# Head norm weight as a row, one product for the output gate, and an earlier start for splitting the feature sums

## The chip, the cores and the metric

The kernel runs on one core of one Trainium2 chip. The metric is the device time of one execution in microseconds (us). Before the change the median of three runs is 1377.43 us (1377.10 to 1377.72).

## The reference

One encoder layer over 1024 tokens of width 1024, in float32. What the change touches is in the first half of it:

```python
h = rmsnorm(x, norm_mix[l])
proj = h @ w_in[l]
q, k, v, r, lr_f, lr_b, u, g_a, g_b = jnp.split(proj, split_points, axis=-1)
...
o = o_fwd + o_bwd                                   # gated linear attention, 4 heads of 256 values
o = o * lax.rsqrt(jnp.mean(o * o, axis=-1, keepdims=True) + EPS)
o = o.transpose(0, 2, 1, 3).reshape(bsz, length, GLA_VALUE_DIM) * gla_norm[l].astype(jnp.float32)
o = (o * jax.nn.silu(r.astype(jnp.float32))).astype(x.dtype)
y_a = o @ w_branch_gla[l]
```

After it come a pooling branch, a gated merge of the two branches, an output projection, and a SwiGLU feed-forward part.

## The kernel before

**Number format.** Every large product is made of three: each float32 operand is split into a high part, which ScalarE rounds (`split_to`, L201, names ending in `h`), and a low part, the difference, which VectorE or GpSimd subtracts (L202, names ending in `l`). TensorE then adds high times high, high times low and low times high into one PSUM bank (L274).

**Order of the work.** The program is written by hand, in the order in which each engine runs it. `pump` (L162) is called once per three products and counts them. A list of generators stands beside the main line, and each is advanced when its count has run down. `beside` (L685) is one of them: at each step it issues loads (SyncE's queue), casts a high part (L708, `trh`) for the job of the step before, and subtracts the low part (L699, `trl`) of the cast before that. What a step yields is the number of product triples until its next step.

**Stages around the change.** The attention of head h runs beside the projections. When one half of the tokens of a head is done, `turn` (L991) multiplies each token's row of `o` (token on the partition, 256 values in the row) by that token's norm (L997), transposes blocks of 32 by 32 on VectorE (L998) and stores the result to DRAM (`o_out`). The projection of r follows, feature tile by feature tile, j from 0 to 5, with two halves of 512 tokens each; one half is 24 products of TensorE. For each (j, half), `gated` (L1199) takes the silu of r on ScalarE (L1202, `sr`) and multiplies it with the loaded `o` (`ol`) and with the norm's weight, which there is one number per partition (L1212). That product is cut into four instructions of 128x128. Four gated pieces make a block that is stored to DRAM (`ob_out`).

The tiles j = 6 and 7 of r, and the later projections, are computed by a seven-product scheme for 2 x 2 blocks (`Unit`, L1090, and `Gates`, L1475). The first unit runs its products in the order p = 1, 2, 6, 5, 3, 7, of 12 TensorE products each. Its products 1, 2 and 3 use the split activations `hh` and `hl`, which are in SBUF. Products 6, 5, 7 and 4 use sums of activation blocks, which were stored to DRAM earlier (`f_out`). `feature_parts` (L666) loads these eight sums (two for each p, in the order p = 6, 5, 7, 4; `hs`) and lets `beside` split them into `trh` and `trl`. The weights of the unit are loaded as `fraw`; for p = 1 and 2 they are split as they are, for the other p sums of them (`fs`, L1110) are made on VectorE first. Product 6 adds onto the PSUM bank of product 1, so it waits until ScalarE has copied product 1 out (L1497, `ga`).

**Memory.** Nearly all tiles of 512 KB (4 KB per partition) take turns in one pool of 39 slots: a tile's first writer waits for the last reader of the tile that had the slot before.

Of the kernel before, what the change touches and what calls it, by code (L numbers as in the profile page):

```python
# [10 lines left out]
F32 = mybir.dt.float32  # L11
# [4 lines left out]
ALU = mybir.AluOpType  # L16

P = 128
# [7 lines left out]
DV = 256  # L26
# [3 lines left out]
SQ = 32  # L30
# [14 lines left out]
PUT = 3  # L45
# [9 lines left out]
def kernel(  # L55
# [20 lines left out]
    nc = tc.nc  # L76
# [4 lines left out]
    const = ctx.enter_context(tc.tile_pool(name="const", bufs=1))  # L81
# [12 lines left out]
    def name(s):  # L94
        count[0] += 1
        return f"{s}_{count[0]}"

    def slot(dtype=F32, shape=(2, HALF), s="slot"):
        return slots.tile([P, *shape], dtype, tag="slot", name=name(s))

    def t2(width=HALF, dtype=F32, s="t"):
        return tmp.tile([P, width], dtype, tag="t2", name=name(s), padded_shape=[P, HALF + 2 * PAD])
# [7 lines left out]
    def bank(pool, s="ps"):  # L110
        return pool.tile([P, HALF], F32, tag=pool.name, name=name(s))

    def as_f32(ap):
        return ap.bitcast(F32)
# [33 lines left out]
    side, aside = [], []  # L148
# [6 lines left out]
    def soon(delay, *steps):  # L155
        put_off.extend([delay, step] for step in steps)
# [283 lines left out]
    g_mix, g_ffn, g_gla, g_pool = (cols[:, 8 * i : 8 * i + 8] for i in range(4))  # L440
# [118 lines left out]
    def later(dst, src):  # L559
        deferred.append((dst, src))  # L560

    def flush(eng=nc.sync):
        while deferred:
            eng.dma_start(*deferred.pop(0))
# [101 lines left out]
    def feature_parts():  # L666
        todo = [(p, c) for p in (6, 5, 7, 4) for c in range(2)]
        wholes = []

        def load_sum():  # L670
            if len(wholes) < len(todo):
                p, c = todo[len(wholes)]
                wholes.append(slot(s="hs"))
                nc.sync.dma_start(wholes[-1][:, :, :], f_out[p][:, c])

        yield load_sum, None, None
        for n, (p, c) in enumerate(todo):
            yield load_sum, wholes[n][:, :, :], p

    def parts_for(src):  # L680
        if len(src.shape) == 2:
            return [t2(dtype=F32R, s=s)[:, :] for s in ("uph", "upl")]
        return [slot(F32R, s=s)[:, :, :] for s in ("trh", "trl")]

    def beside(jobs, every, put, lag):  # L685

        casts, differ = [None] * lag, None
        puts = [[] for _ in range(put)]
        while True:
            job = next(jobs, None)  # L690
            if not any((job, *casts, differ, *puts)):
                return
            if put:
                for pair in puts.pop(0):
                    nc.sync.dma_start(*pair)
            puts.append([])
            if differ:
                src, (hi, lo), dst = differ
                nc.vector.tensor_tensor(lo, src, as_f32(hi), op=ALU.subtract)  # L699
                if len(src.shape) == 2:  # L700
                    puts[-1] += [(dst[:, i, :], as_f32(t)) for i, t in enumerate((hi, lo))]
                else:
                    right.setdefault(dst, []).append((hi, lo))
            differ, cast = None, casts.pop(0)
            if cast:
                src, dst = cast
                parts = parts_for(src)
                nc.scalar.copy(parts[0], src)  # L708
                differ = src, parts, dst
            casts.append(None)  # L710
            if job:
                op, src, dst = job
                if op:
                    op()
                if src is not None:
                    casts[-1] = src, dst
                elif dst is not None:

                    puts[-1].append((dst, op.args[0]))
            if not put:  # L720
                for pair in puts.pop():
                    nc.sync.dma_start(*pair)
            yield every

    def prepare_beside(jobs, every, put=PUT, lag=1):
        aside.append([beside(chain(*jobs), every, put, lag), every])

    def finish_beside():
        while aside:
# [5 lines left out]
    o_heads, unscaled, last_o = {}, [], []  # L735
# [78 lines left out]
    def attention(h):  # L814
# [113 lines left out]
        def scores(half):  # L928
            sc = [bank(ps_g, "sc") for _ in range(2)]
            for d in range(2):  # L930
                for i in range(4):
                    n = 4 * half + i
                    nc.tensor.matmul(
                        sc[d][:, i * CH : (i + 1) * CH], chunk_of(ke, n, d), chunk_of(qe, n, d),
                        start=True, stop=True,
                    )
            hi, lo = (t2(dtype=F32R, s="p")[:, :] for _ in range(2))
            nc.vector.copy_predicated(sc[1][:, :], keep.rearrange("p n c -> p (n c)"), sc[0][:, :])
            split_to(hi, lo, sc[1][:, :])
            return hi, lo  # L940
# [41 lines left out]
        p = scores(0)  # L982
# [5 lines left out]
        old = sf = None  # L988
        scales, turned = {}, {}

        def turn(half, part):  # L991
            if part == 0:
                turned[half] = slot(shape=(DV // SQ, 4 * SQ), s="ot")
            two = slice(2 * part, 2 * part + 2)
            for i in range(2 * part, 2 * part + 2):
                t = o[half][:, i, :]
                nc.vector.tensor_scalar(t, t, scales[half][:, i : i + 1], None, op0=ALU.mult)  # L997
            nc.vector.transpose(  # L998
                turned[half][:, :, :].rearrange("p k (n b) -> p n k b", b=SQ)[:, two],
                o[half][:, two, :].rearrange("p n (k a) -> p n k a", a=SQ),  # L1000
            )
            if part:
                to = o_out[h][half].rearrange("(k a) (i m) -> i a k m", a=SQ, i=4)
                for i in range(4):
                    (last_o if h == HEADS - 1 else deferred).append((to[i], turned[half][i * SQ : (i + 1) * SQ, :, :]))

        for n in range(NT):
            half, i = n // 4, n % 4
            op = bank(ps_g, "op")
# [21 lines left out]
            if n == 3:  # L1031
                p = q_next
# [166 lines left out]
    def gated(j, half, src):  # L1199

        sr = t2(s="sr")
        nc.scalar.activation(sr[:, :], src, AF.Silu)  # L1202
        if j // 2 not in oT:
            oT[j // 2] = [slot(s="o") for _ in range(2)], []
        tiles, there = oT[j // 2]

        def every(t, i):
            return t.rearrange("p (n i b) -> p i n b", n=4, b=SQ)[:, i]

        turned = o_heads[j // 2][half][:, j % 2, :].rearrange("p (i n b) -> p i n b", i=4, b=SQ)  # L1210
        for i in range(4):
            nc.vector.scalar_tensor_tensor(  # L1212
                every(tiles[half][:, j % 2, :], i), turned[:, i], g_gla[:, j : j + 1], every(sr[:, :], i),
                op0=ALU.mult, op1=ALU.mult,
            )
        there.append((j, half))
        if len(there) == 4:
            c = j // 2 % 2
            for half, t in enumerate(tiles):
                later(ob_out[j // 4, half][:, 2 * c : 2 * c + 2, :], t[:, :, :])  # L1220
            soon(2, flush)
# [8 lines left out]
    for j in range(KT - 2):  # L1230
        if 2 <= j <= 4:
            load_o(j - 2)
        w = take()
        if j == 4:
            for _ in range(2):
                gunits[0].load()
        if j == 5:
            gates_ahead.step()
        if j < BY:
            whole_r = slot(s="r")  # L1240
        for half in range(2):
            if j >= BY and not sums_begun and (j > BY or not side):
                finish_side()
                finish_beside()
                prepare_beside([feature_parts()], 5)
                sums_begun = True
            ps = feature_major(w, hT, half)
            if half == 0:
                flush()
                if j == 4:  # L1250
                    deferred.extend(last_o)
                    flush()
                elif j == 5:
                    load_o(HEADS - 1)
            elif j == KT - 3:
                for _ in range(2):
                    gunits[1].load()
            if j < BY:
                nc.scalar.copy(whole_r[:, half, :], ps[:, :])
                raw_r.append((j, half, whole_r[:, half, :]))  # L1260
            else:
                put_by()
                gated(j, half, ps[:, :])
            if j == KT - 3 and half == 0:
                gates_ahead.step()
# [746 lines left out]
    scales = {}  # L2012
# [74 lines left out]
    for at, p in enumerate(OUT_ORDER):  # L2087
# [9 lines left out]
        for i in range(CLOSE if closing else n_of):  # L2097
            n = at * n_of + i
# [57 lines left out]
```

## Time and profile before

| what | value |
|---|---|
| median of three runs | 1377.43 us |
| the profiled execution's own time | 1377.28 us |
| its span, first to last instruction | 1375.6 us |
| TensorE (PE) busy | 1357.9 us, 99% of the span |
| VectorE (DVE) busy | 861.7 us |
| ScalarE (ACT) busy | 647.2 us |
| GpSimd (POOL) busy | 756.6 us |
| mean granted clock of TensorE | 0.995 |

All times below are microseconds from the start of the span. In a timeline row stand the start, the duration, the engine, the line, the operation, what is written and read, and how many instructions are merged into the row; in square brackets the idle time of the engine before it and what ended it. PE is TensorE, SPq the queue of SyncE that issues the DMAs.

### The profile page before, as it was taken

What the parts mean: (1) busy time and instruction counts of PE and PEld (TensorE: products, weight loads), DVE (VectorE), ACT (ScalarE), POOL (GpSimd) and SP (SyncE); (2) the same over time, 40 slices, a digit from 0 to 9 for tenths busy, and PEclk for the clock granted to TensorE, in tenths of its full rate; (3) what the DMA queues carried; (4) which work ended last, traced back from release to release, by engine and by line L of the source; (5) the groups of instructions that cost most, each with busy time, mean ns of one, the idle gap of its engine ahead of it and who ended that gap; (6) DMA issues with size and microseconds to landing.
All of it is one profiled execution on the core that took longest, in us unless ns stands there. A gap on an engine that the chain in (4) does not pass through costs nothing. (4 is left out here: it accounts for less than half of the span.)

```text
span 1375.6 us, 17848 instructions
## 1 busy us (share of the span) xinstructions
PE 1357.9 (99%) x6246; PEld 1129.0 (82%) x6246; DVE 861.7 (63%) x1102; ACT 647.2 (47%) x1177; POOL 756.6 (55%) x561
## 2 busy tenths in 40 slices
PE   9999999999799999999999999999999999999998
PEld 7888888888688888888888888888888888888886
DVE  6965556657745777688883955656556556343375
ACT  7365666754434445554347533333333334444353
POOL 3323723222487547668665376666666667455454
PEclk9999999999899999999999999999999999999999
DMA  6322523315778578996416355555544447985552
GB/s 226 115 85 55 184 84 93 91 48 170 259 230 281 183 217 302 374 369 221 165 62 245 115 177 176 177 176 177 170 143 136 143 139 266 386 305 185 170 214 77
DMA packets 176987, 254.08 MB, mean 185 GB/s; under 512 B 11608, under 2 KB 102784, under 8 KB 176896
## 3 DMA queue, kind: packets, MB, share of 16 engines
q1 hardware_dynamic: 176752, 252.67, 54.7%
q8 instruction: 49, 0.80, 0.2%
q14 instruction: 42, 0.34, 0.1%
q10 hardware_dynamic: 144, 0.26, 0.0%
HBM read 169.79 MB, written 83.10 MB: 184 GB/s over the span
## 5 line engine op out<-in xcount | busy, mean ns | idle before, releaser
L202 POOL TENSOR_TENSOR wl<-fs,wh 128x512 fp32r<-128x512 f32 x124 | 173.8, 1406 | 163.3 <-ACT wh L201 107.2
L274 PE MATMUL ps<-gh,wh 128*128 128x512 f32 x616 | 240.5, 390 | 0.0
L274 PE MATMUL ps<-gl,wh 128*128 128x512 f32 x616 | 239.8, 389 | 0.3 <-DVE gl L1714 0.3
L274 PE MATMUL ps<-gh,wl 128*128 128x512 f32 x616 | 239.7, 389 | 0.0
L202 POOL TENSOR_TENSOR wl<-fraw,wh 128x512 fp32r<-128x512 f32 x93 | 135.4, 1456 | 74.4 <-ACT wh L201 70.0
L202 POOL TENSOR_TENSOR ol<-gor,oh 128x1024 fp32r<-128x1024 f32 (+1 forms) x42 | 101.6, 2423 | 85.7 <-ACT oh L201 71.1
L274 PE MATMUL ps<-hh,wh 128*128 128x512 f32 x356 | 144.3, 405 | 0.7 <-ACT ga L1497 0.7
L274 PE MATMUL ps<-hl,wh 128*128 128x512 f32 x356 | 138.8, 390 | 0.0
L274 PE MATMUL ps<-hh,wl 128*128 128x512 f32 x356 | 138.8, 390 | 0.0
L274 PEld LDWEIGHTS ps<-gl,wh 128*128 128x128 f32 x616 | 115.7, 188 | 24.3 <-DVE gl L1714 0.7
L274 PEld LDWEIGHTS ps<-gh,wl 128*128 128x128 f32 x616 | 115.6, 188 | 24.2
L274 PEld LDWEIGHTS ps<-gh,wh 128*128 128x128 f32 x616 | 115.7, 188 | 24.0 <-ACT hb L1733 0.3
L274 PE MATMUL ps<-oh,oh 128*128 128x512 f32 x308 | 119.8, 389 | 0.0
L274 PE MATMUL ps<-ol,oh 128*128 128x512 f32 x308 | 119.8, 389 | 0.0
L274 PE MATMUL ps<-oh,ol 128*128 128x512 f32 x308 | 119.8, 389 | 0.0
L202 POOL TENSOR_TENSOR wl<-wraw,wh 128x512 fp32r<-128x512 f32 x56 | 93.4, 1696 | 44.3 <-ACT wh L201 44.2
L202 DVE TENSOR_TENSOR ol<-wor,oh 128x1024 fp32r<-128x1024 f32 (+1 forms) x42 | 62.6, 1501 | 67.8 <-ACT oh L201 55.3
L202 POOL TENSOR_TENSOR wl<-raw,wh 128x512 fp32r<-128x512 f32 x34 | 47.9, 1419 | 85.6 <-ACT wh L201 62.1
L201 ACT CAST wh<-fs 128x512 fp32r<-128x512 f32 x124 | 76.0, 614 | 29.7 <-DVE fs L1110 28.7
L274 PEld LDWEIGHTS ps<-hh,wl 128*128 128x128 f32 x356 | 66.8, 188 | 14.1
L274 PEld LDWEIGHTS ps<-hh,wh 128*128 128x128 f32 x356 | 67.0, 188 | 13.4 <-ACT ga L1497 1.1
L274 PEld LDWEIGHTS ps<-hl,wh 128*128 128x128 f32 x356 | 67.0, 188 | 12.3
(278 smaller groups left out, 3091.1 us busy)
## 6 DMA issues: line engine op xcount, KB each, us to landing
fraw<-in_w_ffn_in_dram SPq DMA_DIRECT2D x44, 512.0 KB, 6.9
gor<-g_out SPq DMA_DIRECT2D x35, 512.0 KB, 7.1
fraw<-in_w_in_dram SPq DMA_DIRECT2D x22, 512.0 KB, 7.5
g_out<-s SPq DMA_DIRECT2D x44, 256.0 KB, 2.0
wor<-t_out SPq DMA_DIRECT2D x20, 512.0 KB, 5.2
raw<-in_w_in_dram SPq DMA_DIRECT2D x36, 256.0 KB, 4.5
g_out<-g SPq DMA_DIRECT2D x33, 256.0 KB, 2.6
x<-in_x_dram SPq DMA_DIRECT2D x16, 512.0 KB, 4.4
```

The source lines that it names most:

```text
L201: nc.scalar.copy(hi, src)
L202: eng.tensor_tensor(lo, src, as_f32(hi), op=ALU.subtract)
L274: nc.tensor.matmul(ps, a[i], b[j], start=first and n == 0, stop=last and n == 2, skip_group_check=onto)
```

## The change

Three edits:

1. `turn` multiplies by the norm's weight too. Each head loads a tile `gain_row`, its 256 weights broadcast to all 128 partitions, by one more DMA; the `tensor_scalar` of L997 becomes a `scalar_tensor_tensor` with that row. The count of instructions stays (32 of 128x256).
2. `gated` has no weight to multiply any more, and its four `scalar_tensor_tensor` of 128x128 become one `tensor_tensor` of 128x512. There are 16 gated pieces, so 64 instructions become 16.
3. The `beside` generator that splits the feature sums takes its first two steps one product triple apart, where all its steps were five apart. Its first step comes after one triple, not five, and all later steps come twelve triples earlier in the program.

```diff
-    def beside(jobs, every, put, lag):
+    def beside(jobs, every, put, lag, quick):
...
-            yield every
-
-    def prepare_beside(jobs, every, put=PUT, lag=1):
-        aside.append([beside(chain(*jobs), every, put, lag), every])
+            quick -= 1
+            yield 1 if quick >= 0 else every
+
+    def prepare_beside(jobs, every, put=PUT, lag=1, quick=0):
+        aside.append([beside(chain(*jobs), every, put, lag, quick), 1 if quick else every])
...
+        gain_row = const.tile([P, DV], F32, tag="gain_row", name=name("gain_row"))
+        nc.sync.dma_start(gain_row[:, :], gla_norm[0:1, h * DV : (h + 1) * DV].broadcast_to([P, DV]))
+
         def turn(half, part):
...
-                nc.vector.tensor_scalar(t, t, scales[half][:, i : i + 1], None, op0=ALU.mult)
+                nc.vector.scalar_tensor_tensor(
+                    t, t, scales[half][:, i : i + 1], gain_row[:, :], op0=ALU.mult, op1=ALU.mult
+                )
...
-        def every(t, i):
-            return t.rearrange("p (n i b) -> p i n b", n=4, b=SQ)[:, i]
-
-        turned = o_heads[j // 2][half][:, j % 2, :].rearrange("p (i n b) -> p i n b", i=4, b=SQ)
-        for i in range(4):
-            nc.vector.scalar_tensor_tensor(
-                every(tiles[half][:, j % 2, :], i), turned[:, i], g_gla[:, j : j + 1], every(sr[:, :], i),
-                op0=ALU.mult, op1=ALU.mult,
-            )
+        turned = o_heads[j // 2][half][:, j % 2, :].rearrange("p (i n b) -> p n i b", i=4, b=SQ)
+        dst, silu = (t.rearrange("p (n i b) -> p n i b", n=4, b=SQ) for t in (tiles[half][:, j % 2, :], sr[:, :]))
+        nc.vector.tensor_tensor(dst, turned, silu, op=ALU.mult)
...
-                prepare_beside([feature_parts()], 5)
+                prepare_beside([feature_parts()], 5, quick=2)
```

The third edit moves instructions on ScalarE and in SyncE's queue. The first place is ScalarE's order between r's fourth tile and the first unit. `trh<-hs` is the cast of a feature sum, `sr` a silu for a gated piece, `wh<-fraw` the cast of the unit's weights for p = 1 and then p = 2. The number behind a name tells tiles apart. Before:

```order
L708 CAST trh_3467<-hs_3400 128x1024
L1202 ACTIVATE sr_3483<-r_2882 128x512
L1202 ACTIVATE sr_3489<-ps_3435 128x512
L708 CAST trh_3511<-hs_3462 128x1024
L1202 ACTIVATE sr_3528<-r_2882 128x512
L1202 ACTIVATE sr_3534<-ps_3497 128x512
L201 CAST wh_3540<-fraw_3431 128x512
L708 CAST trh_3549<-hs_3470 128x1024
L708 CAST trh_3572<-hs_3514 128x1024
L1202 ACTIVATE sr_3587<-r_3015 128x512
L1202 ACTIVATE sr_3593<-ps_3544 128x512
L201 CAST wh_3599<-fraw_3431 128x512
```

With the change, from the third sum's cast on:

```order
L708 CAST trh_3472<-hs_3403 128x1024
L1208 ACTIVATE sr_3491<-r_2888 128x512
L1208 ACTIVATE sr_3494<-ps_3444 128x512
L708 CAST trh_3507<-hs_3424 128x1024
L708 CAST trh_3528<-hs_3475 128x1024
L1208 ACTIVATE sr_3536<-r_2888 128x512
L1208 ACTIVATE sr_3539<-ps_3499 128x512
L201 CAST wh_3542<-fraw_3440 128x512
L708 CAST trh_3562<-hs_3510 128x1024
L1208 ACTIVATE sr_3583<-r_3021 128x512
L1208 ACTIVATE sr_3586<-ps_3546 128x512
L201 CAST wh_3589<-fraw_3440 128x512
```

The cast of the fourth sum (`trh_3572` before, `trh_3507` now) stood behind the p = 1 weights' cast and now stands ahead of it; ahead of the p = 2 weights' cast there were four sums' casts and now there are six. What follows on ScalarE now, up to the copy of product 1 that product 6 waits for, are the casts of the last two sums, two silus, three casts of weight sums and the copy:

```order
L708 CAST trh_3602<-hs_3531 128x1024
L708 CAST trh_3621<-hs_3565 128x1024
L1208 ACTIVATE sr_3634<-r_3021 128x512
L1208 ACTIVATE sr_3637<-ps_3597 128x512
L201 CAST wh_3647<-fs_3595 128x512
L201 CAST wh_3651<-fs_3593 128x512
L201 CAST wh_3661<-fs_3655 128x512
L1497 COPY ga_3681<-ps_3667 128x512
```

The last two sums' casts stood behind that copy before, and stand ahead of it now.

The second place is SyncE's queue in the same stretch. Before:

```order
L674 DMA hs_3514<-f_out_562 128x1024
L674 DMA hs_3552<-f_out_564 128x1024
L564 DMA ob_out_2777<-o_3370 128x1024
L564 DMA ob_out_2778<-o_3371 128x1024
L674 DMA hs_3575<-f_out_564 128x1024
L1050 DMA ol_3583<-o_out_568 128x2x512
L1050 DMA ol_3584<-o_out_568 128x2x512
L674 DMA hs_3621<-f_out_561 128x1024
L674 DMA hs_3642<-f_out_561 128x1024
```

With the change:

```order
L674 DMA hs_3510<-f_out_564 128x1024
L674 DMA hs_3531<-f_out_561 128x1024
L564 DMA ob_out_2783<-o_3378 128x1024
L564 DMA ob_out_2784<-o_3379 128x1024
L674 DMA hs_3565<-f_out_561 128x1024
L1056 DMA ol_3579<-o_out_568 128x2x512
L1056 DMA ol_3580<-o_out_568 128x2x512
```

The last two sums' loads (`f_out_561`) stood behind the load of `ol` and now one stands ahead of the stores `ob_out` and one right behind them.

## The prediction, made before the changed kernel was run

> **What bounds the kernel now.** I read the page first, then the waits of TensorE, then the stretch with the only long wait.
>
> ```profile
> PE 1357.9 (99%) x6246; PEld 1129.0 (82%) x6246; DVE 861.7 (63%) x1102; ACT 647.2 (47%) x1177; POOL 756.6 (55%) x561
> ...
> PE ps L274 <- ACT ga L1497: 7.9, 2, 7.2
> PE op L274 <- DVE p L202: 0.4, 2, 0.2
> ```
>
> TensorE has work for 1357.9 of 1375.6 us. Its largest wait is one of 7.2 us for the copy `ga`; the other of that row (0.7 us) is product 3's wait for the copy of product 5, which the order 5, 3 makes in both kernels. The change can win what this one stall costs and little else. The timeline of TensorE and the windows around it (PE and PEld busy, DVE, ACT, POOL; then the granted clock):
>
> ```profile
> 346.81 0.39 PE L274 MATMUL ps<-hh,wh 128*128 128x512 f32 x1
> 347.04 0.39 PE L274 MATMUL ps<-hl,wh 128*128 128x512 f32 x1
> 347.27 0.39 PE L274 MATMUL ps<-hh,wl 128*128 128x512 f32 x1
> ...
> 351.80 0.39 PE L274 MATMUL ps<-hl,wh 128*128 128x512 f32 x1
> 352.03 0.39 PE L274 MATMUL ps<-hh,wl 128*128 128x512 f32 x1
> 359.66 0.79 PE L274 MATMUL ps<-trh,wh 128*128 128x512 f32 x1 [7.25 <-ACT ga L1497]
> 360.25 0.63 PE L274 MATMUL ps<-trl,wh 128*128 128x512 f32 x1
> 360.68 0.63 PE L274 MATMUL ps<-trh,wl 128*128 128x512 f32 x1
> ...
> 365.37 0.47 PE L274 MATMUL ps<-trl,wh 128*128 128x512 f32 x1
> ...
> 352.20:359.70 7.50, 0.25 (x2) 0.04 (x1) 6.41 (x12) 4.10 (x8) 3.04 (x3) 0.71 1.09 356
> 359.70:365.40 5.70, 5.70 (x14) 4.44 (x15) 2.93 (x6) 3.59 (x6) 5.12 (x3) 0.50 0.85 340
> ```
>
> TensorE's products follow each other by 0.227 us; the 24 of the unit's p = 1 and p = 2 run from 346.81 to 352.26. Product 6 could have started at 352.26 and started at 359.66: 7.4 us. Then the clock stands at 0.50, and products from 360.25 to 365.37 follow by 0.427 us: 13 times 0.2 us, 2.6 us more. The stall is worth 10 us, 0.7%.
>
> Who is late is seen on ScalarE:
>
> ```profile
> 336.63 0.61 ACT L201 CAST wh<-fraw 128x512 fp32r<-128x512 f32 x1
> 337.14 1.05 ACT L708 CAST trh<-hs 128x1024 fp32r<-128x1024 f32 x1
> 344.06 1.05 ACT L708 CAST trh<-hs 128x1024 fp32r<-128x1024 f32 x1 [5.88 <-PE ps L274]
> 345.02 0.63 ACT L1202 ACTIVATE sr<-r 128x512 f32<-128x512 f32 x1
> 345.55 0.58 ACT L1202 ACTIVATE sr<-ps 128x512 f32<-128x512 f32 x1
> 346.03 0.61 ACT L201 CAST wh<-fraw 128x512 fp32r<-128x512 f32 x1
> ...
> 352.02 1.05 ACT L708 CAST trh<-hs 128x1024 fp32r<-128x1024 f32 x1 [3.68 <-DMA hs<-f_out]
> ...
> 358.50 0.62 ACT L201 CAST wh<-fs 128x512 fp32r<-128x512 f32 x1 [3.40 <-DVE fs L1110]
> 359.03 0.58 ACT L1497 COPY ga<-ps 128x512 f32<-128x512 f32 x1
> ```
>
> The copy is short and its input, product 1, is done at 349.5 (346.81 and 12 times 0.227); it stands at the end of a queue that waited for a slot (344.06), for a load (352.02) and for VectorE (358.50). VectorE was late through gated pieces and GpSimd:
>
> ```profile
> 353.63 4.24 DVE L1212 SCALAR_TENSOR_TENSOR o<-ol,cols,sr 128x128 f32<-128x128 f32 x8 [1.09 <-ACT sr L1202]
> ...
> L1212 DVE SCALAR_TENSOR_TENSOR o<-ol,cols,sr 128x128 f32<-128x128 f32 x64 | 28.6, 516 | 13.2 <-ACT sr L1202 10.6 <-POOL wl L202 2.4
> ...
> 358.39 0.68 DVE L1110 TENSOR_TENSOR fs<-fraw,fraw 128x512 f32<-128x512 f32 x1
> 358.99 1.21 DVE L699 TENSOR_TENSOR trl<-hs,trh 128x1024 fp32r<-128x1024 f32 x1
> ```
>
> **The gate as one product.** 64 instructions hold VectorE 28.6 us in this stretch. A 128x512 product of two SBUF tensors takes 0.68 us and the next starts after 0.60 (358.39 to 358.99). 16 of them are 10.9 us: VectorE gets 17.7 us back. The operands' runs stay 32 numbers long; were each product no faster than four old ones at their median of 0.344 us, it would take 1.4 us and still lengthen nothing. By itself this would bring `fs` and the copy nearer, by about 2.9 us of the 4.24 at 353.63. Whether it does depends on what ScalarE waits for.
>
> **The row weight.** No row shows a `scalar_tensor_tensor` of 128x256 from SBUF. The nearest are the old form and the same form from PSUM:
>
> ```profile
> L997 DVE TENSOR_SCALAR o<-o,ors x32: 310/344/1395, 125.7 to 323.6; 128x256 f32<-128x256 f32 x32
> L917 DVE SCALAR_TENSOR_TENSOR st<-kv,fac,so x48: 445/483/486, 97.4 to 317.3; 128x256 f32<-128x256 f32 x48
> ```
>
> So 0.10 to 0.14 us more each, 32 of them: 3.2 to 4.5 us of VectorE from 125 to 325. I cost this at nothing: TensorE works on the projections beside the attention and waits there for VectorE 0.4 us in all, 0.2 at most (the row `op` above). Without that cover it costs up to 4.5 us. Four more DMAs of 128 KB in SyncE's queue are issued long before the first use; behind them stand loads and stores of tiles needed much later. Zero.
>
> **The earlier sums.** The loads, casts and low parts come twelve triples, 8 us, earlier in the program. That gains only where nothing else holds them, and two things do.
>
> First, the slot at 344.06. The fourth sum's cast takes a slot that r's last half-tile (TensorE) still reads; the built program has it wait for the same matmul in both kernels. In the new order the cast of the p = 1 weights, which before ran at 336.63, stands behind it: two casts (0.96 each from start to start), two silus (0.53, 0.48), so it starts at 346.99 and ends at 347.6. TensorE wants it at 346.81: 0.8 us late. Its low part on GpSimd takes 1.29 us more, to 348.9, or to 350.3 if VectorE's low part is ahead of it, where the third product of p = 1 stood at 347.27. **A new stall of 1.6 to 3.1 us opens in front of the old one.** It costs nothing in the sum as long as product 6 still waits longer. The p = 2 weights follow a load that can issue at 344.29 only:
>
> ```profile
> 342.70 0.34 SPq L674 DMA_DIRECT2D hs<-f_out  x1
> 343.09 0.90 SPq L564 DMA_DIRECT2D ob_out<-o  x2
> ...
> 344.29 1.10 SPq L674 DMA_DIRECT2D hs<-f_out  x1
> ...
> DMA to landing us min/median/max: 2.6/3.5/4.4
> ...
> L564 SPq DMA_DIRECT2D ob_out<-o x8: 338/424/3318, 343.1 to 389.8; - x8
> ...
> DMA to landing us min/median/max: 2.6/7.0/8.1
> ```
>
> The first landing row is of the sums' tiles, loads and earlier stores together; the second, with the row above it, is of the `ob_out` stores. With 3.5 us the p = 2 cast runs at 349.8 to 350.4; p = 2 begins at 351.1 to 352.6. In time. Products 1 and 2 end at 353.9 to 355.4.
>
> Second, and this sets product 6: the seventh sum's cast (`trh_3602`) takes the slot of a gated block, and waits until the second `ob_out` store has read it. That store waits for the gated product of the silu at 345.98, done at 347.3, so it issues at 347.4. Its landing takes 2.6 to 8.1 us by the last row; the queue ahead of it is as at 342.70 (a sum's load and a store), with less behind it, so I take 6.4, nearer to the loaded median than to the store that ran alone: **353.8**. From there it is serial, since the eighth cast takes the slot that the seventh low part frees: cast 1.05, low part 1.21, cast 0.96, silu 0.63, on VectorE two gated products and two weight sums (0.60, 0.60, 0.60, 0.68), copy 0.58, releases 0.2: 7.1 us. Product 6 starts at 360.9, 1.2 us later than before.
>
> Its third product needs the low part of its weights. GpSimd is asked for it 4.9 us after the landing, while VectorE runs five two-input instructions without a pause:
>
> ```profile
> 365.91 0.68 DVE L1110 TENSOR_TENSOR fs<-fraw 128x512 f32<-128x512 f32 x1
> 366.51 1.22 DVE L699 TENSOR_TENSOR trl<-hs,trh 128x1024 fp32r<-128x1024 f32 x1
> 367.65 0.68 DVE L1110 TENSOR_TENSOR fs<-fs,fraw 128x512 f32<-128x512 f32 x1
> ...
> 366.37 3.10 POOL L202 TENSOR_TENSOR wl<-fraw,wh 128x512 fp32r<-128x512 f32 x1 [1.55 <-ACT wh L201]
> 369.43 1.29 POOL L202 TENSOR_TENSOR wl<-fs,wh 128x512 fp32r<-128x512 f32 x1
> ```
>
> At 366.37 GpSimd took 3.10 us for what takes 1.29 alone: it got on when VectorE's row ended at 368.3. Blocked so until 361.3, the low part ends at 362.6, 1.9 us after the old 360.68; if it slips in between, the lateness stays 1.2. I take 1.5. [...]
>
> **The sum**, on the profiled execution's 1377.28 (its median of three runs is 1377.43, 0.15 higher): gate 0, row 0, sums +1.5, clock as before 0: **1378.8 us, +0.1%**. Measurement here tells 0.2%, 2.75 us, from no change, so I call it no change: the stall moves from a load to a store. Bounds of the term: the store at 2.6 us, with ScalarE free from 350.4, gives 357.5, 2.2 us sooner; 8.1 us gives 362.6 and with the blocked GpSimd 3.6 later.
>
> **Rivals.**
> - *The stall goes* (0.05). If the casts' slots come free earlier than I read from the built program, all eight sums are split before 352. 1377.3 - 7.4 - 2.6 = 1367.3. For it: VectorE has the time. Against: the 5.88 us wait at 344.06, which an earlier request only lengthens.
> - *The store lands quickly* (0.12). 2.6 us, 2.2 gained; the idle stretch is then too short for the slow clock, 2.6 more: 1372.5. Against: two more transfers leave within 1 us of it.
> - *The clock stays up* (0.20). My idle stretch is 5.5 to 7 us, broken by the two halves of the new stall, against 7.4 in one piece, of which the clock at 0.71 says that it fell after about 3 (3.1 us at 1 and 4.4 at 0.5 make 0.71). Without the slow products 1378.8 - 2.6 = 1376.2, still no change. [...]
> - *The store is late: slower* (0.16). At 8.1 us, GpSimd blocked: 1377.3 + 3.6 = 1380.9. It decides from a landing of 7.4 us on (354.8, plus 8.8 to the third product, 2.9 late). For it: the median of 7.0 is close.
> - *The longer row instruction reaches TensorE* (0.05): up to 1377.3 + 4.5 = 1381.8. Against: no wait of TensorE on VectorE above 0.2 us there.
>
> My forecast itself has 0.42. Faster: 0.17 (the first two). Same: 0.42 + 0.20 = 0.62. Slower: 0.21. The range 1373.0 to 1381.3 leaves out the vanished stall, about half of the quick store and the top of the last.
>
> **What would show it.** Right: TensorE idle in two places, some 0.8 us at 346.8 and 1 to 2 us right behind it, released by the p = 1 weights (`wh`, then `wl`), where it had no gap; then 5 to 7 us up to about 361, released by the copy or by `wl`; ScalarE waiting at 344.06 with the p = 1 cast after it, and for an `ob_out` store near 353.8; gated products of 0.68 us, VectorE's total some 14 us lower. Wrong: no gap at 346.8; product 6 before 357 or after 363; a gap of TensorE above 1 us before 340.

## The result, and the profile after

The changed kernel takes 1383.41 us (median of five runs, 1383.05 to 1384.54), the kernel before, on the same chip, 1377.43 (1377.10 to 1377.79). The ratio is 1.0046, 95% interval 1.0031 to 1.0060: **slower by 6.0 us**, where I had forecast 1378.8 and a range up to 1381.3. The profiled execution of the change took 1384.49 us, its span is 1382.7 (1375.6 before); it is 1.1 us above its median.

The busy times on the page of the changed kernel:

```profile
PE 1358.9 (98%) x6246; PEld 1128.5 (82%) x6246; DVE 857.4 (62%) x1054; ACT 647.3 (47%) x1177; POOL 754.5 (55%) x561
```

Its waits of TensorE (us in total, times, longest):

```profile
PE ps L274 <- ACT ga L1497: 10.7, 2, 9.9
PE ps L274 <- POOL wl L202: 2.3, 4, 0.9
...
PE ps L274 <- ACT wh L201: 0.7, 1, 0.7
```

TensorE is busy for 1358.9 us (1357.9 before): of the 7.1 us between the two spans 1.0 is busy time, and the rest is waiting. The wait for the copy `ga` has grown from 7.2 to 9.9 us, and there are small waits for weights, `wl` and `wh`, that were not there. The timeline of TensorE in r's stage, after the change:

```profile
349.28 0.50 PE L274 MATMUL ps<-hh,wh 128*128 128x512 f32 x1 [0.67 <-ACT wh L201]
...
350.76 0.50 PE L274 MATMUL ps<-hh,wl 128*128 128x512 f32 x1 [0.75 <-POOL wl L202]
...
366.71 0.80 PE L274 MATMUL ps<-trh,wh 128*128 128x512 f32 x1 [9.94 <-ACT ga L1497]
```

Product 6 starts at 366.71, where it started at 359.66. ScalarE's timeline shows the order that it waits through:

```profile
345.70 2.01 ACT L708 CAST trh<-hs 128x1024 fp32r<-128x1024 f32 x2 [9.57 <-PE ps L274]
...
348.62 0.61 ACT L201 CAST wh<-fraw 128x512 fp32r<-128x512 f32 x1
349.70 1.05 ACT L708 CAST trh<-hs 128x1024 fp32r<-128x1024 f32 x1 [0.47 <-DMA hs<-f_out]
...
357.38 1.04 ACT L708 CAST trh<-hs 128x1024 fp32r<-128x1024 f32 x1 [5.11 <-DMA ob_out<-o]
359.72 1.04 ACT L708 CAST trh<-hs 128x1024 fp32r<-128x1024 f32 x1 [1.29 <-DVE trl L699]
...
364.32 0.62 ACT L201 CAST wh<-fs 128x512 fp32r<-128x512 f32 x1 [1.52 <-DVE fs L1116]
366.07 0.59 ACT L1497 COPY ga<-ps 128x512 f32<-128x512 f32 x1 [1.13 <-DVE fs L1116]
```

The casts at 345.70 are the fourth and fifth of the sums, then come the sixth (349.70), the seventh (357.38) and the eighth (359.72), and only then the copy. Before, the seventh and eighth stood behind it:

```profile
359.03 0.58 ACT L1497 COPY ga<-ps 128x512 f32<-128x512 f32 x1
...
360.03 1.05 ACT L708 CAST trh<-hs 128x1024 fp32r<-128x1024 f32 x1
...
361.50 1.04 ACT L708 CAST trh<-hs 128x1024 fp32r<-128x1024 f32 x1
```

Of the 7.05 us by which product 6 is later, 1.64 are there already at the fourth cast (345.70 to 344.06). Most of those are one wait of TensorE in the attention:

```profile
167.52 0.50 PE L274 MATMUL ps<-wl,hh 128*128 128x512 f32 x1 [0.94 <-POOL wl L202]
```

The profile of before has no wait there, but it isn't the row's: the runs below with the gate alone and with the sums alone have it too (0.69 and 1.06 us), and the row alone has no more of it (0.63). What is left, 5.4 us, arises between the fourth cast and product 6.

### The profile page after: what moved, and what is told of

It is laid out like the page before. It is cut to its first block, busy times and chain, and to the rows that moved or that the text cites. A ratio compares the mean times of both kernels' runs of the same rounds, so it can differ in the third digit from the quotient of the medians.

```text
span 1382.7 us, 17799 instructions
## 1 busy us (share of the span) xinstructions
PE 1358.9 (98%) x6246; PEld 1128.5 (82%) x6246; DVE 857.4 (62%) x1054; ACT 647.3 (47%) x1177; POOL 754.5 (55%) x561
## 5 line engine op out<-in xcount | busy, mean ns | idle before, releaser
L274 PE MATMUL ps<-trh,wh 128*128 128x512 f32 x176 | 69.6, 396 | 9.9 <-ACT ga L1497 9.9
```

The lines of the kernel that those rows point to most:

```text
L274: nc.tensor.matmul(ps, a[i], b[j], start=first and n == 0, stop=last and n == 2, skip_group_check=onto)
```

## The experiments

All times are medians; each ratio is to the kernel before, timed on the same chip (1377.5 to 1377.75), with its 95% interval.

### The three parts apart

**The row alone:** the changed kernel, sums as before, the gate in its four old pieces with a constant.

```diff
-                every(tiles[half][:, j % 2, :], i), turned[:, i], g_gla[:, j : j + 1], every(sr[:, :], i),
+                every(tiles[half][:, j % 2, :], i), turned[:, i], 1.0, every(sr[:, :], i),
```

> The kernel before with the head norm's weight as a row alone: the row is loaded and multiplied in as the head's output is scaled, the gate stays in four pieces with the constant 1 in place of the weight, the sums begin as before. Theory A (the loss lies in the sums that begin early; the row adds a little in the attention): 1377.7 to 1379.0, the 32 row instructions at 0.44 to 0.48 us, TensorE's stall in r's stage still 7 to 7.5 us. Theory B (the row instruction on VectorE is what costs: it holds GpSimd off and pushes the whole program back): 1381 or more. Theory C (nothing): within 0.3 of 1377.4.

Measured: 1377.69, ratio 1.0002 (0.9993 to 1.0012). Theory B is out; A and C are inside the interval. The row's only trace is a wait of TensorE in the attention, here in the changed kernel, for ScalarE's `sf`; `sf` is made from `st`, which VectorE makes behind the row's instructions:

```profile
194.26 0.48 PE L1026 MATMUL op<-sf,qe 128*128 128x256 f32 x1 [0.37 <-ACT sf L922]
```

Without the row (before, gate alone, sums alone) the gap at this place is 0.11 us. So 0.26 us are shown, and the rest isn't told from nothing.

**The gate alone,** without the head norm's weight:

```diff
-        for i in range(4):
-            nc.vector.scalar_tensor_tensor(...)
+        nc.vector.tensor_tensor(dst, turned, silu, op=ALU.mult)
```

> The kernel before with the gate as one 128x512 product alone; the head norm's weight is left out of the computation, so that nothing else differs. Theory A (VectorE's two gated blocks of 4.24 us were in front of the weight sum that the copy waits behind): the weight sum starts up to 2.9 us sooner, the stall of 7.2 us becomes 4.3 to 5, 1373 to 1375. Theory B (each whole product gives GpSimd its turn, so that the weight sums take 1.75 instead of 0.68 us): the gain is 2.9 less 2.1, 1376.3 to 1377.0. Theory C (ScalarE's load and slot set the end anyway): 1377.4.

Measured: 1375.83, ratio 0.9988 (0.9979 to 0.9998), 1.7 us less. The stall is 5.2 us, between A and B in size, and the weight sums take the 1.75 us of B. VectorE's timeline in this kernel:

```profile
354.29 1.29 DVE L1209 TENSOR_TENSOR o<-ol,sr 128x512 f32<-128x512 f32 x2 [1.75 <-ACT sr L1202]
355.50 1.75 DVE L1110 TENSOR_TENSOR fs<-fraw,fs 128x512 f32<-128x512 f32 x1
357.18 1.75 DVE L1110 TENSOR_TENSOR fs<-fraw,fraw 128x512 f32<-128x512 f32 x1
```

and GpSimd's:

```profile
355.32 4.74 POOL L202 TENSOR_TENSOR wl<-fs,wh 128x512 fp32r<-128x512 f32 x3 [6.33 <-ACT wh L201]
```

The two gated blocks went from 4.24 to 1.29 us. But now the two weight sums `fs` run beside GpSimd's three low parts, and take 1.75 us each where they took 0.68. From the first gated block to the end of the first `fs` it was 4.84 us (353.63 to 357.79 and 0.68) and is 2.96 (354.29 to 355.50 and 1.75): 1.9 us gained of the 2.95 that the blocks gave up.

**The sums alone:** the early start, gate and weight as before.

```diff
-                prepare_beside([feature_parts()], 5)
+                prepare_beside([feature_parts()], 5, quick=2)
```

> The kernel before with the earlier sums alone: the first two steps of the sums follow r's fourth tile at once, gate and weight as before. Theory A (the sums are the loss: the cast of the p = 1 weights and the seventh sum's cast, which waits for a store): 1381 to 1384, two small stalls at about 347 and then one of 8 to 10 us ended by the copy. Theory B (it is the row, or the gate's meeting with GpSimd): 1376.5 to 1378.5.

Measured: 1383.67, ratio 1.0047 (1.0030 to 1.0064). Theory A: the sums alone cost as much as the whole change. The stall ends where it does in the change:

```profile
366.93 0.80 PE L274 MATMUL ps<-trh,wh 128*128 128x512 f32 x1 [11.10 <-ACT ga L1499]
```

and with the old gate VectorE's `fs` are short again:

```profile
360.74 4.24 DVE L1214 SCALAR_TENSOR_TENSOR o<-ol,cols,sr 128x128 f32<-128x128 f32 x8 [1.64 <-ACT sr L1204]
364.90 0.68 DVE L1112 TENSOR_TENSOR fs<-fraw,fs 128x512 f32<-128x512 f32 x1
365.50 0.68 DVE L1112 TENSOR_TENSOR fs<-fraw,fraw 128x512 f32<-128x512 f32 x1
```

**Row and gate, no early sums:**

```diff
-                prepare_beside([feature_parts()], 5, quick=2)
+                prepare_beside([feature_parts()], 5)
```

> The changed kernel with the sums begun as before: row and gate together. Theory A: the sum of the two runs before it (row 0.3 to 1.6, gate 0 to -4): 1373.5 to 1378.5, and no stall before the p = 1 products. Theory B (the row or the gate carries the loss): 1381 or more.

Measured: 1376.26, ratio 0.9990 (0.9981 to 1.0000): the sum of the two single runs (+0.2 and -1.7), within their intervals. Against this kernel the early sums cost 7.1 us (1383.41 less 1376.26).

### What in the sums costs

**The late weights of product 1** (`p = 1`), split one tile of r earlier:

```diff
         if j == 4:
             for _ in range(2):
                 gunits[0].load()
-        if j == 5:
             gates_ahead.step()
```

> The changed kernel with the weights of the unit's first product (p = 1) split one tile of r earlier, ahead of the sums. Theory A (the two gaps of 0.7 and 0.8 us at 348 to 351 come from the p = 1 cast behind two casts of sums, and are covered by the later stall): the gaps are gone, the later stall begins 1.4 us sooner and ends at the same time, 1383.4 within 0.5. Theory B (what is lost in the gaps is lost for good): 1.4 less, 1382.0.

Measured: 1383.99, ratio 1.0047 (1.0032 to 1.0062). The waits at product 1 are gone but for 0.16 us; two of 0.64 and 0.74 stand in front of product 2 instead. Product 6 starts at 366.48 all the same. The small gaps cost nothing while the long stall stands behind them: theory A, except that the gaps moved.

**The store that the seventh cast waits for.** A quarter of each of the first two blocks is stored first, and as many bytes as the rest has follow from another tile, so that this kernel leaves out three quarters of their gated output:

```diff
-                later(ob_out[j // 4, half][:, 2 * c : 2 * c + 2, :], t[:, :, :])
+                dst, w = ob_out[j // 4, half][:, 2 * c : 2 * c + 2, :], HALF // 4 if j < 2 else HALF
+                later(dst[:, :, :w], t[:, :, :w])
+            for half in range(2 * (j < 2)):
+                later(ob_out[0, half][:, 0:2, w:], as_f32(hT.pair(0, 0)[0][:, :, :])[:, :, w:])
```

> The changed kernel with the first two ob_out stores cut in two: a quarter of each block is stored first, and the other three quarters of the place are filled from another tile (that part of the gated output is left out), so that as many bytes move but the slots of the blocks are free after a quarter. Theory A (the store is only the first of two holds: behind it the eighth cast waits for its load, which lands at 359.0 whatever the store does): the seventh cast starts 3 us or more sooner than 357.4, the eighth at 359.1, product 6 0.6 us sooner, 1382.5 to 1383. Theory B (the landing of the store alone sets product 6): 3.5 to 4 us sooner, 1379.5.

Measured: 1382.88, ratio 1.0038 (1.0023 to 1.0053). ScalarE's timeline of this kernel:

```profile
352.89 1.05 ACT L708 CAST trh<-hs 128x1024 fp32r<-128x1024 f32 x1 [0.83 <-DMA hs<-f_out]
358.19 1.04 ACT L708 CAST trh<-hs 128x1024 fp32r<-128x1024 f32 x1 [4.26 <-DMA hs<-f_out]
```

The seventh cast runs 4.5 us sooner, the eighth 1.5, and product 6 starts at 365.19, 1.5 us sooner (0.3 of it the program brings along up to there); the median is 0.5 lower. Theory A: behind the store there is a second hold, the load of the eighth sum. A late store alone doesn't explain the loss.

**The seventh and eighth cast out of the way.** The first attempt held back the step that casts the seventh sum, and with it all behind it, by 8 triples:

```diff
-            yield 1 if quick >= 0 else every
+            yield 1 if quick >= 0 else every + 8 if quick == -6 else every
```

> The whole change, with the sums begun early as in it, but the seventh step of the sums held back by 8 more units of time, so that the copy of product 1 is queued after the seventh cast and ahead of the eighth, and the silus and weights ahead of both. Theory A (the sums cost by two casts, the seventh and the eighth, which are not wanted before product 4 and now stand ahead of the copy; the start of the first ones costs nothing): the copy follows the landing of the ob_out store at 357.3 by 1.1 us, product 6 starts at 359 to 359.7, 1376.0 to 1377.5, the small gaps at 348 to 351 still there. Theory B (the early start itself costs, by the late weights of p = 1 and p = 2 and the loads that wait in SyncE's queue): 1381 to 1383.5.

Measured: 1384.05, ratio 1.0048 (1.0033 to 1.0063), but the run decides nothing: the line is shared by every queue of prepared work, and all of them were held. Product 6 did start at 360.70, after a stall of 3.7 us, and two waits for pooled halves just behind 552 us, of 3.0 and 0.7 us, took as much. The longer one:

```profile
PE yb L274 <- DMA ph<-p_out: 3.0, 1, 3.0
```

The same hold for the sums' queue alone (`held` is true for it only):

```diff
+        casts, differ, held = [None] * lag, None, quick == 2
...
+            yield 1 if quick >= 0 else every + 8 if held and quick == -6 else every
```

> The hold of the seventh step of the sums by 8 units again, for the sums' queue alone. Theory A (the two casts ahead of the copy are the loss): product 6 at 360 to 361 in place of 366.7, with an idle stretch under 4 us, and nothing given back later: 1376.0 to 1378.0. Theory B (the early start itself costs): 1381 to 1383.5.

Measured: 1377.48, ratio 1.0000 (0.9990 to 1.0009). ScalarE's timeline:

```profile
358.16 0.62 ACT L201 CAST wh<-fs 128x512 fp32r<-128x512 f32 x1 [1.68 <-DVE fs L1116]
358.68 1.04 ACT L708 CAST trh<-hs 128x1024 fp32r<-128x1024 f32 x1
359.63 0.58 ACT L1497 COPY ga<-ps 128x512 f32<-128x512 f32 x1
```

and TensorE's:

```profile
360.26 0.50 PE L274 MATMUL ps<-trh,wh 128*128 128x512 f32 x1 [3.67 <-ACT ga L1497]
```

The sums still begin early, the waits at 348 to 351 are still there, and the loss is gone: 5.9 us come back by what stands in front of the copy. Theory A. Of the 7.1 us against row and gate alone 1.2 are left; the intervals of the two runs are some 1.3 us to either side, so these runs don't show whether the early start itself costs anything.

**One early step in place of two:**

```diff
-                prepare_beside([feature_parts()], 5, quick=2)
+                prepare_beside([feature_parts()], 5, quick=1)
```

> The changed kernel with one early step of the sums in place of two. Theory A (the loss comes as soon as the seventh and eighth casts stand ahead of the copy, which one step already does): most of the loss, 1380 to 1383. Theory B (each early step costs its share): half of it, 1379.5 to 1380.

Measured: 1381.24, ratio 1.0027 (1.0017 to 1.0038). A's number: five of the seven us are lost already (1381.24 less 1376.26). Both casts are ahead of the copy (355.50 and 362.70, the copy at 363.65). But 2.2 us of the waiting stand in front of product 2 here, for its `wh`, so the run is less clean than the one before it.

### What is between GpSimd and VectorE

The low parts of the first unit's weights on VectorE:

```diff
-            split_to(hi, lo, src, nc.gpsimd)
+            split_to(hi, lo, src, nc.vector if self is gunits[0] else nc.gpsimd)
```

> The changed kernel with the low parts of the first unit's weights on VectorE in place of GpSimd. Theory A (the weight sums took 1.75 in place of 0.68 us because GpSimd's low parts came between, and shut VectorE out): the sums fs at 362 to 365 take 0.68, two low parts of 0.68 stand among them, the copy comes 0.5 to 1 us sooner, 1382.4 to 1383. Theory B (something else slows VectorE there, the transfers for one): fs still 1.7, and the low parts as slow, 2 us later, 1385.

Measured: 1383.90, ratio 1.0047 (1.0030 to 1.0064). VectorE:

```profile
361.56 1.29 DVE L202 TENSOR_TENSOR wl<-fs,wh 128x512 fp32r<-128x512 f32 x2
362.76 0.69 DVE L1116 TENSOR_TENSOR fs<-fraw,fs 128x512 f32<-128x512 f32 x1
364.13 0.69 DVE L202 TENSOR_TENSOR wl<-fs,wh 128x512 fp32r<-128x512 f32 x1 [0.68 <-ACT wh L201]
364.74 0.69 DVE L1116 TENSOR_TENSOR fs<-fraw,fraw 128x512 f32<-128x512 f32 x1
```

The `fs` take 0.69 us here, theory A's number, where they took 1.75 with the low parts on GpSimd. How the two engines come to delay each other is not shown. The time is no better, since three low parts and a wait of 0.68 us for a cast now stand between the gated blocks and the second `fs`.

### A version that is faster than both

If the copy at the end of ScalarE's queue is what TensorE waits for, work that doesn't need the copy should be put there. Product 6 adds onto product 1's bank and needs it; product 5 begins a bank of its own.

```diff
-    R_RUN = 1, 2, 6, 5, 3, 7, 4
+    R_RUN = 1, 2, 5, 6, 3, 7, 4
...
-        todo = [(p, c) for p in (6, 5, 7, 4) for c in range(2)]
+        todo = [(p, c) for p in (5, 6, 7, 4) for c in range(2)]
```

On row and gate:

> Row and gate as in the change, sums begun as before (1376.3), and product 5 ahead of product 6 in the unit of r, with the sums taken in that order. Theory A (TensorE stalls only because product 6 adds onto product 1's bank and so needs the copy at ScalarE's end; product 5 starts a bank of its own and needs its weights alone, cast some 3 us before the copy): product 5 runs inside the stall, 2.7 us less, 1373.6; if both pieces of idle time are then too short for the slow clock, up to 2.6 us less again, 1371.0. Theory B (all weights and sums there are late, not the copy): 1376.3.

On the kernel before:

> The kernel before with product 5 ahead of product 6 alone. Theory A: product 5 starts at about 354.8, 4.9 us sooner than product 6 did; product 6 follows at 359.8; 2.7 us less, 1374.8, and with the clock kept up 1372.1. Theory B: 1377.4.

On the whole change:

> The changed kernel with product 5 ahead of product 6. Theory A (the first of the late weights is cast at 361.7, the copy comes at 366.1): product 5 at 362.3 to 365.1, product 6 at 366.7 as before, 2.7 us less, 1380.7; the idle time ahead of product 5 is still 6 us, so the clock still falls. Theory B (the weights are as late as the copy): 1383.4.

Measured: 1373.71, ratio 0.9972 (0.9961 to 0.9983); 1373.63, 0.9972 (0.9962 to 0.9983); 1382.31, 1.0036 (1.0024 to 1.0047). Product 5 ran inside the stall in all three, and the gains are 2.5, 3.9 and 1.1 us. A had 2.7 for each, and more with the clock kept up, which it was not (0.50 again from 357 to 362 us in the first and from 361 to 367 in the third; a mean of 0.80 from 350 to 360 in the second). Row and gate add nothing to the order (the first two are alike): product 5 waits for its weights on ScalarE, not for VectorE. In the third, product 5 starts at 361.79, and product 3 now waits 1.6 us for a copy `ga`, until 372.10, where it waited 0.7 us in the changed kernel. That doesn't explain the small gain: the profiled execution has this wait and still took 1380.84 us, about A's time. The seven times of this kernel lie apart, three from 1380.84 to 1381.15, one at 1382.31 and three from 1383.12 to 1383.40, and why they do is open.

Then product 5's weights were split one step earlier, ahead of the casts that wait for a load, on row and gate with the new order:

```diff
             if j == KT - 3 and half == 0:
                 gates_ahead.step()
+                gates_ahead.step()
...
-    for _ in range(AHEAD - 2):
+    for _ in range(AHEAD - 3):
```

> Row and gate as in the change, the sums begun as before, product 5 ahead of product 6 (1373.7), and the weights of product 5 split one step earlier, ahead of the sums' casts that wait for a load. Theory A (the rest of the stall is the weights' cast at ScalarE's end): product 5 follows product 2 without a gap, product 6 waits 1 to 2 us for the copy, 4 us less, 1369.7; with the slow clock still coming, 1371 to 1372. Theory B (the weights wait for VectorE and GpSimd all the same): 1373.7.

Measured: **1371.84, ratio 0.9958 (0.9943 to 0.9973)**, 5.9 us less than before the change. TensorE in this kernel:

```profile
353.65 0.39 PE L274 MATMUL ps<-hh,wl 128*128 128x512 f32 x1
353.88 0.39 PE L274 MATMUL ps<-trh,wh 128*128 128x512 f32 x1
...
356.37 0.39 PE L274 MATMUL ps<-trh,wl 128*128 128x512 f32 x1
359.23 0.50 PE L274 MATMUL ps<-trh,wh 128*128 128x512 f32 x1 [2.47 <-ACT ga L1498]
359.56 0.39 PE L274 MATMUL ps<-trl,wh 128*128 128x512 f32 x1
```

Product 5 (from 353.88) follows product 2 without a gap, the stall is 2.5 us, and the products after it follow by 0.23 us: the clock stays up (granted 1.00 in each of four windows from 353 to 369 us). That is A's time with the slow clock, got without the slow clock: product 6 waits 2.47 us where A had 1 to 2, and product 3 waits for another copy (0.92 us).

With the low parts on VectorE as well (the diff of the section above):

> The best version (1371.8) with the low parts of the first unit's weights on VectorE. Theory A (what is left of the stall is the weight sums at 1.76 us, shut out by GpSimd): they take 0.68, but two low parts of 0.60 come before the copy, so 0 to 0.5 us less, 1371.3 to 1371.8. Theory B (VectorE is then late with the low parts of the sums too): 1372.5 or more.

Measured: 1374.20, ratio 0.9974 (0.9964 to 0.9985): theory B, 2.4 us worse than the version without. Product 6's wait fell only from 2.47 to 2.13 us, and product 3's grew from 0.92 to 2.40.

## Why the prediction was wrong

The direction of the term and its mechanism stood; its sizes did not.

**What held.** The stall at product 1: I had 0.8 us for `wh` and 1 to 2 for `wl`, measured 0.67 and 0.75. The fourth cast waits for TensorE in both kernels, as read (9.57 in place of 5.88 us of waiting, `<-PE ps`). The seventh cast waits for an `ob_out` store. The row: costed at 0, measured +0.2. The gated product has a median of 0.69 us in the changed kernel (I took 0.68). The slow clock came as before (0.50 from 361.8 to 372.1 us).

**The landing of the store: taken 6.4 us, measured over 8.** SyncE's timeline in the changed kernel:

```profile
348.43 0.90 SPq L564 DMA_DIRECT2D ob_out<-o  x2
351.85 0.32 SPq L674 DMA_DIRECT2D hs<-f_out  x1
352.42 0.97 SPq L1056 DMA_DIRECT2D ol<-o_out  x2
```

and a window over the stretch (the last two columns are the share of the DMA engines and GB/s):

```profile
346.00:356.90 10.90, 8.94 (x36) 6.11 (x34) 9.47 (x10) 5.80 (x9) 3.19 (x2) 1.00 0.80 248
```

The second store was issued by 349.33, 1.9 us after the 347.4 that I took; 1.64 of that is the lateness that the kernel brings along. The cast that it releases starts at 357.38, 8.05 us later; I had 6.4 and so 353.8, with a bound of 8.1. In the kernel before, a row for the same two stores alone (L564, 342 to 344.5 us) was there to be read:

```profile
DMA to landing us min/median/max: 6.4/7.0/7.5
```

I took its lower end. Why the landing took 8 us is open. Three more transfers of 512 KB were issued from 351.85 on, before the store had landed; but before the change four were issued behind the same stores within 5 us (344.29, two from 345.44, 347.45), and no run took the later ones away.

**The eighth cast's load: not in the sum.** I called all that follows the store serial, with the eighth cast held by a slot. In the changed kernel it is the slot that releases it (1.29 us, `<-DVE trl`), so the sum lost nothing here. But it also needs a load, issued at 351.85: with the store out of the way the seventh cast ran 4.5 us sooner, and the eighth waited 4.26 us for that load. So an early slot for the seventh cast alone does not give the 1372.5 of my rival "the store lands quickly".

**The serial part: taken 7.1 us, measured 9.3** (357.38 to 366.71). VectorE in the changed kernel:

```profile
361.32 1.29 DVE L1215 TENSOR_TENSOR o<-ol,sr 128x512 f32<-128x512 f32 x2 [1.64 <-ACT sr L1208]
362.54 1.75 DVE L1116 TENSOR_TENSOR fs<-fraw,fs 128x512 f32<-128x512 f32 x1
364.21 1.75 DVE L1116 TENSOR_TENSOR fs<-fraw,fraw 128x512 f32<-128x512 f32 x1
```

and GpSimd:

```profile
362.36 4.72 POOL L202 TENSOR_TENSOR wl<-fs,wh 128x512 fp32r<-128x512 f32 x3 [8.23 <-ACT wh L201]
```

The two `fs` took 1.75 in place of 0.68 us, 2.1 of the 2.2 us. I had the right rows, and drew the wrong side of them: from 3.10 us of one low part I concluded that VectorE's row holds GpSimd off, and added 0.3 us for a late low part, for which product 6's third product (367.73) did not wait. That VectorE holds GpSimd off was my estimate from that one row; no run shows it. Here it is VectorE, on the path, that pays more: 2.1 us on two sums, where GpSimd's three low parts take 0.85 us longer than three of the 1.29 us that one took with VectorE idle (373.47). What the runs show is the time: 1.75 us for each of these sums with the low parts on GpSimd, 0.69 with them on VectorE.

**The gate: taken 0 on the path and 17.7 us of VectorE; measured 1.7 us of time and 5.0 of VectorE** (861.7 to 856.7 with the gate alone; 857.4 in the whole change, not some 14 less). The gated products with the gate alone:

```profile
L1209 DVE TENSOR_TENSOR o<-ol,sr 128x512 f32<-128x512 f32 x16 | 13.9, 892 | 17.7 <-ACT sr L1202 16.5 <-POOL wl L202 1.2
```

They went from 28.6 to 13.9 us, where I had 10.9: not all of the 16 took the median's 0.69 us, and their mean is 0.89. The other 9.7 us were lost outside the gate, by VectorE instructions that take longer in this kernel: the weight sums `fs` 6.8 us more over the whole program, `trl` 2.6, `upl` 1.9, with small changes both ways in the rest. The `fs` of r's stage went back to 0.69 us above with the low parts off GpSimd; for the others that was not tested. And by itself the shorter gate did reach the copy. With early sums it gave nothing: the old gate takes 1383.67 there, the new one, with the row, 1383.41.

**The sum again, by what was measured.** The step that failed is the term of the early sums, taken at +1.5. It measured +7.1 on top of row and gate, which are -1.2 together; these two give the 6.0 by construction, since 7.1 is the difference to that kernel. The three single runs give +0.2 - 1.7 + 6.2 = 4.7, no further off than their intervals of 1.3 to 2.3 us to either side allow. On the path as I had described it product 6 was to start at 360.9 and started at 366.71, past the 363 that I had named as a sign of being wrong. The 5.8 us are 1.9 of the store's later issue, 1.7 of its landing, and 2.2 of the serial part. Of the 7.1, 5.9 went when the seventh cast was held to just ahead of the copy and the eighth behind it.

Behind the sizes stands a question that I did not ask. I asked when the seventh cast would run; I did not ask why it should stand ahead of the copy at all, when its sum isn't wanted before product 4. A change that starts a queue of eight jobs twelve triples sooner brings the last two forward as well, and these were what cost.

## What to carry to other kernels

When work on an in-order engine is begun earlier, list what is queued behind each piece of it now and was ahead of it before; the last pieces, not the first, decide, since they jump ahead of something that is wanted sooner. A wait can have a second hold behind it, as the store had the eighth sum's load (4.26 us): before pricing the first, ask what the instruction needs besides. And where TensorE waits for a chain that can't be shortened, look for a product that doesn't need the chain: here two lines of order were worth 3.9 us, where the planned change lost 6.0.

## What the runs showed of the hardware that I had not expected

From the stall of the kernel before I had estimated that the clock falls after about 3 us of idling. In these runs its fall doesn't go with the length of one idle stretch. The version with product 5 first (row and gate) was idle for 1.94 and then 0.56 us, two matmuls between them, and fell to half speed at 356.04, during these two:

```profile
352.60:356.00 3.40, 1.46 (x7) 0.87 (x6) 1.36 (x3) 2.57 (x4) 0.32 (x1) 1.00 1.05 405
356.00:362.90 6.90, 6.34 (x16) 4.52 (x15) 6.81 (x6) 5.09 (x8) 5.56 (x4) 0.51 1.09 354
```

(The columns are as in the prediction: PE's busy time stands behind the length, the granted clock is the third from the end.) With the seventh cast held, TensorE was idle for 3.67 us in one piece. The first products behind that gap still follow by 0.23 us, and the clock fell only after 0.94 us of work:

```profile
357.80:361.20 3.40, 0.94 (x4) 0.81 (x5) 3.40 (x3) 2.57 (x4) 3.40 (x3) 1.00 1.03 341
361.20:364.60 3.40, 3.40 (x10) 2.65 (x9) 3.40 (x3) 1.57 (x2) 2.82 (x2) 0.50 1.11 351
```

In the best version the longest idle stretch there was 2.47 us, and the clock did not fall (1.00 from 353 to 369 us). In the changed kernel it fell at 361.8, some 5.0 us after the last product had ended, and in the kernel before after 2.9:

```profile
351.90:355.30 3.40, 0.51 (x3) 0.09 (x1) 2.31 (x6) 3.08 (x5) 0.64 (x1) 1.00 1.04 400
355.30:365.50 10.20, 5.84 (x14) 4.58 (x15) 7.43 (x12) 4.88 (x8) 7.52 (x5) 0.50 0.96 331
```

The stretch at 0.50 behind each fall, as near as windows of 0.1 us tell, was 10.24 us before (355.28 to 365.52) and 10.24 with the change (361.81 to 372.05). With product 5 first it was 6.8 us (356.04 to 362.9) and with the cast held at least the 3.40 of the last window of its fence. What decides when the clock falls, and for how long, is open: no run moved a gap by itself to test it.
